# Gated product in its own tile, partial sums in `u`, and w_down's work tied to rounds, in a one-core encoder block

## The chip, the cores and the metric

One core of a Trainium2 chip runs the whole program. The metric is the time of one execution on the device in microseconds, the median of several runs. Engines work through their own instruction lists in order and wait for each other by semaphores: TensorE (PE, matmuls), VectorE (DVE), ScalarE (ACT), GpSimd (POOL) and SyncE (SP), whose queue issues the DMAs of this kernel.

## The reference

One layer of a hybrid encoder: token mixing (convolution and attention in parallel), cross-attention into 256 memory tokens, and a gated MLP. Of these the change touches the seam between the cross-attention and the MLP, and the MLP:

```python
h = rmsnorm(x, norm_mem_pre); y = memory_cross_attention(h, mem_n, ...)
x = x + rmsnorm(y, norm_mem_post)
h = rmsnorm(x, norm_ffn_pre)                   # 1024 tokens x 1024
u = jnp.einsum("bsd,df->bsf", h, w_up)         # 1024 x 5632
u = dwconv_centred(u, ffn_dw, ffn_dw_b)        # three taps along the tokens
gate, val = u[..., :D_FF], u[..., D_FF:]       # D_FF = 2816
y = jnp.einsum("bsf,fd->bsd", jax.nn.gelu(gate, approximate=True) * val, w_down)
x = x + rmsnorm(y, norm_ffn_post)
```

All of it is float32; each matmul operand is split into a high and a low part, and a product is three matmuls (high-high, high-low, low-high).

## The kernel before

**The seam.** The last product of the cross-attention runs over 8 token tiles `t` (`cross_gemm`, result `y2` in PSUM). For each tile `cross_norm` makes the two norms: Square on ACT, `rt` and `rs` on POOL (L86, L87), scaling and residual on DVE (L623, L624), Square again, `rt` and `rs` again, and `h` (named `h3` in the code) on DVE (L725). `cross_operands` transposes `h` on PE (`pTs`) and forms from it the moving operands b11, b21, b22, t1 to t4 of the MLP, each with a split into high (`h`) and low (`l`) part; t1 to t4 need the second half of the tokens, thus tile 7.

**The up stage.** There are NF = 22 blocks of 128 gate and 128 value columns, one block a *round* `fi`. A round replaces eight half-products by seven (Strassen's scheme in Winograd's form), p1 to p7, each of 12 matmuls of 128x512. `up_first` makes p1 and p2 from the weights `wg`, split into `a1`; `up_operands` loads `wv`, makes sums `s12` and `s34` on POOL, and splits them into `a2`, `a3`, `a22`; `up_finish` makes p6, p5, p3, p7, p4 and adds them up on DVE into `u` (L836), convolves (`conv3`), applies gelu, and multiplies gate and value (L859) into `u[:, 1]`, which is stored to `act_d[fi]` in DRAM (L860). On PE p1 and p2 of round fi run ahead of p6 to p4 of round fi - 1. Rounds 0 and 1 have their p1 and p2 at the seam (`UP_PRE = 2`).

**w_down's sums.** The down product uses the same scheme on 2x2 blocks; its right-hand sums are made during the up stage: `down_load` loads a slice of w_down into `wd_b` (two slots), `down_sums` makes four subtractions on DVE (L769), `down_store` stores the slice to `T_d` in DRAM (L772).

**The down stage** (`yd`) makes seven products m1 to m7 over 11 pairs `i`; left operands are formed from `acts` (reloaded from act_d), right ones from `st` (a stage of w_down or T_d in a tmp or raw buffer, two `i` each); the split pair is `op`.

**Buffers.** Tiles come from rotating pools; a new tile waits until the last use of the old one is over. `wp` has 7 (a1, a2, a3, a22, u), `tmp` 4 (x2, h3, q, s12, s34), `raw` 3 (wg, wv, x1r), PSUM `psB` 4 banks for p1 to p7, pTs and some yd. The order of instructions on each engine is set by a scheduler that goes by dependencies and its own costs, not by the order in the source alone.

## Time and profile before

| | us |
|---|---|
| median of 3 runs (lowest, highest) | 1452.29 (1451.33, 1456.73) |
| the profiled execution | 1453.6 |
| its span, first to last instruction | 1451.5 |
| PE busy / DVE busy / ACT busy / POOL busy | 1383.5 / 1070.8 / 699.9 / 514.0 |
| first p1 of the up stage | 757.96 |
| first down matmul | 1230.53 |

The profiled execution has 2.1 us ahead of and behind its span. Times within the rows count from the start of the span. A busy PE is not a PE at full speed: the granted clock has two levels, 2.4 and 1.2 GHz, and stands in the windows as a share of the higher. Idle time ahead of an instruction is shown in square brackets with the instruction that ended it.

### The profile page before, as it was taken

To read this page: it belongs to the slowest core of one execution; us is meant where nothing else is said; L and a number is where in the kernel's file an instruction comes from. 1 tells how busy PE (TensorE), PEld (TensorE's weight loads), DVE (VectorE), ACT (ScalarE), POOL (GpSimd) and SP (SyncE) were. 2 spreads that over 40 slices of the span, in tenths; PEclk is the share of its full clock that TensorE was granted. 3 is DMA by queue.
4 is the path that set the end of the run, shared out by engine and by line. 5 is a ranking of instruction groups with operands and counts; after the bars stand their busy time and mean duration, and the time that the engine had idled before them with its cause. 6 is when DMAs were issued, how large, how long until landed. Compare 5 with 4: busy or idle time off the path is not lost.

```text
span 1451.5 us, 18836 instructions
## 1 busy us (share of the span) xinstructions
PE 1383.5 (95%) x7042; PEld 1167.5 (80%) x7042; DVE 1070.8 (74%) x1442; ACT 699.9 (48%) x1191; POOL 514.0 (35%) x506
## 2 busy tenths in 40 slices
PE   9999999799999999999996989789999999999996
PEld 7889988679898888888885767678888888888885
DVE  6699899799998334335458878877777778985576
ACT  7426543588888434334444424234444443544452
POOL 5548887600102324002136525345554441000003
PEclk9999999999999999999998999899999999999998
DMA  6417750000000434013223576742222228622325
GB/s 236 135 59 238 243 200 14 19 1 2 30 1 12 163 103 151 24 43 131 87 87 102 174 232 198 236 135 83 74 93 81 88 87 317 226 88 88 109 87 210
DMA packets 74060, 170.08 MB, mean 117 GB/s; under 512 B 9713, under 2 KB 32497, under 8 KB 73969
## 3 DMA queue, kind: packets, MB, share of 16 engines
q1 hardware_dynamic: 73968, 168.88, 35.1%
q8 instruction: 55, 0.90, 0.3%
q14 instruction: 37, 0.30, 0.1%
HBM read 124.82 MB, written 44.04 MB: 116 GB/s over the span
## 4 chain that ended last, share of the span: by engine, by line
PE 62%; DVE 7%; DMA 5%; ACT 2%; issue 2%; POOL 1%; POOLq 0%; DVEq 0%; ACTq 0%; SPq 0%
PE p L98 7%; PE p L99 6%; PE p L101 6%; PE yd L91 5%; PE yd L92 5%; PE yd L93 5%; PE y L99 4%; PE y L101 4%; PE y L98 4%; PE pPT L82 3%; DVE wd L769 3%; DMA wd<-in_w_down_dram 2%; DMA T_d<-wd 2%; PE sc L101 2%; PE sc L98 2%; PE sc L99 2%
## 5 line engine op out<-in xcount | busy, mean ns | idle before, releaser
L305 DVE SCALAR_TENSOR_TENSOR cacc<-conv,col,cacc 128x1009 f32<-128x1009 f32 (+14 forms) x120 | 145.8, 1276 | 4.7 <-ACT cacc L253 4.5
L86 POOL TENSOR_SCALAR rt<-ss 128x1 f32<-128x1 f32 (+1 forms) x43 | 15.0, 349 | 353.5 <-DVE ss L920 227.2
L92 PE MATMUL yd<-op 128*128 128x512 f32 x308 | 119.8, 389 | 0.0
L93 PE MATMUL yd<-op 128*128 128x512 f32 x308 | 119.7, 389 | 0.0
L775 ACT CAST a<-s 128x512 fp32r<-128x512 f32 x88 | 50.8, 621 | 105.6 <-PE p L101 65.1
L91 PE MATMUL yd<-op 128*128 128x512 f32 x308 | 96.9, 389 | 0.0
L930 ACT CAST op<-acts 128x512 fp32r<-128x512 f32 x77 | 48.0, 624 | 99.6 <-PE yd L93 87.8
L776 POOL TENSOR_TENSOR a<-wg,a 128x512 fp32r<-128x512 f32 x44 | 63.1, 1456 | 84.1 <-ACT a L775 84.0
L920 DVE TENSOR_TENSOR op<-acts,op 128x512 fp32r<-128x512 f32 x77 | 53.1, 690 | 46.5 <-ACT op L930 46.4
L826 DVE SCALAR_TENSOR_TENSOR c<-u,col,c 128x1023 f32<-128x1023 f32 x44 | 56.6, 1285 | 39.9 <-ACT c L825 39.9
L557 DVE TENSOR_TENSOR PL<-pPT,PH 128x512 fp32r<-128x512 f32 x128 | 83.2, 681 | 2.4 <-ACT PH L556 1.4
L539 DVE TENSOR_REDUCE nm<-sp 128x1 f32<-128x1024 f32 x64 | 78.0, 1218 | 7.3 <-PE sp L537 6.8
L825 ACT ACTIVATE c<-u,col 128x1024 f32<-128x1024 f32 x44 | 53.2, 1209 | 54.8 <-DVE u L836 53.4
L542 ACT ACTIVATE P<-sp,nm 128x1024 f32<-128x1024 f32 x64 | 72.2, 1128 | 15.4 <-PE pPT L82 6.5
L776 DVE TENSOR_TENSOR a<-s,a 128x512 fp32r<-128x512 f32 x88 | 67.0, 779 | 15.2 <-ACT a L775 15.0
L556 ACT CAST PH<-pPT 128x512 fp32r<-128x512 f32 x128 | 69.4, 593 | 13.9 <-PE pPT L82 13.4
L769 DVE TENSOR_TENSOR wd<-wd 128x256 f32<-128x256 f32 x88 | 57.0, 664 | 20.5 <-DMA wd<-in_w_down_dram 20.0
L82 PE MATMUL pPT<-ident,P 128*128 128x128 f32 x512 | 67.9, 273 | 0.7 <-DVE PL L557 0.7
L92 PEld LDWEIGHTS yd<-op 128*128 128x128 f32 x308 | 57.8, 188 | 12.4 <-DVE op L920 0.4
L91 PEld LDWEIGHTS yd<-op 128*128 128x128 f32 x308 | 57.8, 188 | 12.0
L93 PEld LDWEIGHTS yd<-op 128*128 128x128 f32 x308 | 57.8, 188 | 12.0
L776 POOL TENSOR_TENSOR a<-wv,a 128x512 fp32r<-128x512 f32 x22 | 32.9, 1513 | 97.5 <-ACT a L775 83.1
(344 smaller groups left out, 4395.1 us busy)
## 6 DMA issues: line engine op xcount, KB each, us to landing
wg<-in_w_up_dram SPq DMA_DIRECT2D x22, 512.0 KB, 4.4
wv<-in_w_up_dram SPq DMA_DIRECT2D x22, 512.0 KB, 4.2
wd<-in_w_down_dram SPq DMA_DIRECT2D x22, 512.0 KB, 4.2
T_d<-wd SPq DMA_DIRECT2D x22, 512.0 KB, 3.9
act_d<-u SPq DMA_DIRECT2D x22, 512.0 KB, 2.9
acts<-act_d SPq DMA_DIRECT2D x22, 512.0 KB, 6.8
st<-T_d SPq DMA_DIRECT2D x20, 512.0 KB, 3.7
wmkv_r<-in_w_mkv_dram SPq DMA_DIRECT2D x16, 512.0 KB, 4.1
```

The source lines that it names most:

```text
L82: nc.tensor.transpose(out=out_, in_=in_, identity=ident)
L91: nc.tensor.matmul(out=ps, lhsT=sh, rhs=mh, start=first, stop=False)
L92: nc.tensor.matmul(out=ps, lhsT=sh, rhs=ml, start=False, stop=False)
L93: nc.tensor.matmul(out=ps, lhsT=sl, rhs=mh, start=False, stop=last)
L98: nc.tensor.matmul(out=p, lhsT=sh, rhs=mh, start=first, stop=False)
L99: nc.tensor.matmul(out=p, lhsT=sh, rhs=ml, start=False, stop=False)
L101: ins = nc.tensor.matmul(out=p, lhsT=sl, rhs=mh, start=False, stop=last)
L305: nc.vector.scalar_tensor_tensor(out=acc[:, t0:t1_], in0=a[:, t0 + o:t1_ + o], scalar=cc(C_DW + c * 31 + j), in1=acc[:, t0:t1_], op0=ALU.m ...
L539: nc.vector.reduce_max(out=nm, in_=sp, axis=AX.X, negate=True)
L557: nc.vector.tensor_tensor(out=PL[dst], in0=p3, in1=f(PH[dst]), op=ALU.subtract)
L769: nc.vector.tensor_tensor(out=dst, in0=in0, in1=in1, op=ALU.subtract)
L776: eng.tensor_tensor(out=dst[:, 1, :], in0=src, in1=f(dst[:, 0, :]), op=ALU.subtract)
```

## The change

- The product of gate and value goes into a tmp tile `o`, from which it is stored; `u` has its last use in that multiplication.
- The partial sums `q` lie in the second half of `u` instead of a tmp tile.
- w_down: the load of a round is issued behind the load of that round's `wv`; its four sums go behind the addition of p7 of the round ahead (`issue_after`), its store behind a later load of the w_up weights.
- The `wv` of rounds 0 and 1 are loaded into one tile `wv2` of the w pool ahead of the last tile's norm; the splits of `a1` for rounds 0 and 1 and the sums of round 0 come ahead of it as well; that norm gets high priority; the subtraction t3 of tile 7 moves from POOL to DVE.

```diff
@@ -624,9 +624,11 @@
         nc.vector.tensor_tensor(out=t, in0=t, in1=resid, op=ALU.add)
         return t
 
+    last_load = [None]
+
     def load_raw(src, name):
         r = raw(name)
-        nc.sync.dma_start(out=r, in_=src)
+        last_load[0] = nc.sync.dma_start(out=r, in_=src)
         return r
 
@@ -715,7 +717,7 @@
-    def cross_norm(t, y, xr):
+    def cross_norm(t, y, xr, eng=None):
...
     def cross_operands(t, j):
+        third = nc.gpsimd if t < 7 else nc.vector
         h, tt = t // 4, t % 4
         ts_ = slice(tt * 128, tt * 128 + 128)
         if t == 4:
@@ -743,7 +746,7 @@
             b_sub("t1", "b12", "b11", ts_, nc.vector)
             b_split("t1", ts_)
             b_split("b22", ts_)
-            b_sub("t3", "b22", "b12", ts_, nc.gpsimd)
+            b_sub("t3", "b22", "b12", ts_, third)
             b_sub("t2", "b22", "t1", ts_, nc.vector)
             b_split("t2", ts_)
             b_split("t3", ts_)
@@ -761,19 +764,22 @@
         return dr[fi // 2, :, :, fi % 2 * 256:fi % 2 * 256 + 256]
 
     def down_load(fi):
-        nc.sync.dma_start(out=wd_b[:, fi % 2], in_=down_slice(w_down, fi))
-
-    def down_sums(fi):
+        with tc.issue_after(last_load[0].ins):
+            nc.sync.dma_start(out=wd_b[:, fi % 2], in_=down_slice(w_down, fi))
+
+    def down_sums(fi, behind):
         b11, b12, b22, b21 = [wd_b[:, fi % 2, b, :] for b in range(4)]
-        for dst, in0, in1 in ((b11, b12, b11), (b12, b22, b12), (b22, b22, b11), (b21, b22, b21)):
-            nc.vector.tensor_tensor(out=dst, in0=in0, in1=in1, op=ALU.subtract)
+        with tc.issue_after(behind.ins):
+            for dst, in0, in1 in ((b11, b12, b11), (b12, b22, b12), (b22, b22, b11), (b21, b22, b21)):
+                nc.vector.tensor_tensor(out=dst, in0=in0, in1=in1, op=ALU.subtract)
 
     def down_store(fi):
-        nc.sync.dma_start(out=down_slice(T_d, fi), in_=wd_b[:, fi % 2])
+        with tc.issue_after(last_load[0].ins):
+            nc.sync.dma_start(out=down_slice(T_d, fi), in_=wd_b[:, fi % 2])
 
     def a_split(dst, src, eng):
         nc.scalar.copy(out=dst[:, 0, :], in_=src)
-        eng.tensor_tensor(out=dst[:, 1, :], in0=src, in1=f(dst[:, 0, :]), op=ALU.subtract)
+        return eng.tensor_tensor(out=dst[:, 1, :], in0=src, in1=f(dst[:, 0, :]), op=ALU.subtract)
 
     def product(ps, a, b):
         bh, bl = BO[b]
@@ -785,39 +791,56 @@
     H0, H1 = slice(0, 512), slice(512, 1024)
     ups, firsts, rgs = {}, {}, {}
 
-    def up_first(fi):
-
+    a1s, rvs, sums = {}, {}, {}
+    UP_PRE = 2
+
+    def up_first_operands(fi):
         rg = rgs.pop(fi) if fi in rgs else load_raw(w_up[fi, 0], "wg")
         a1 = W([2, 2, 512], "a1")
         a_split(a1[:, 0], rg[:, H0], nc.gpsimd)
         a_split(a1[:, 1], rg[:, H1], nc.gpsimd)
+        a1s[fi] = rg, a1
+
+    def up_first(fi):
+
+        if fi not in a1s:
+            up_first_operands(fi)
+        rg, a1 = a1s[fi]
         u = wp.tile([128, 2, 1024], F32, tag="w", name="u")
-        q = tmp("q")
+        q = u[:, 1, :]
         p1, p2 = psB("p1"), psB("p2")
         product(p1, a1[:, 0], "b11")
         nc.scalar.copy(out=q[:, H0], in_=p1)
         product(p2, a1[:, 1], "b21")
         nc.vector.tensor_tensor(out=u[:, 0, H0], in0=p2, in1=q[:, H0], op=ALU.add)
-        firsts[fi] = (rg, u, q)
-
-    def up_operands(fi):
-
-        rg, u, q = firsts.pop(fi)
-        rv = load_raw(w_up[fi, 1], "wv")
+        firsts[fi] = (u, q)
+
+    def up_sums(fi):
+        rg, _ = a1s.pop(fi) if fi >= UP_PRE else a1s[fi]
+        rv = rvs.pop(fi) if fi in rvs else load_raw(w_up[fi, 1], "wv")
         s12, s34 = tmp("s12"), tmp("s34")
         nc.gpsimd.tensor_tensor(out=s12[:, H0], in0=rv[:, H0], in1=rv[:, H1], op=ALU.add)
         nc.gpsimd.tensor_tensor(out=s12[:, H1], in0=s12[:, H0], in1=rg[:, H0], op=ALU.subtract)
         nc.gpsimd.tensor_tensor(out=s34[:, H0], in0=rg[:, H0], in1=rv[:, H0], op=ALU.subtract)
         nc.gpsimd.tensor_tensor(out=s34[:, H1], in0=rg[:, H1], in1=s12[:, H1], op=ALU.subtract)
+        sums[fi] = rv, s12, s34
+
+    def up_operands(fi):
+
+        if fi not in sums:
+            up_sums(fi)
+        rv, s12, s34 = sums.pop(fi)
+        u, q = firsts.pop(fi)
         a2, a3 = W([2, 2, 512], "a2"), W([2, 2, 512], "a3")
         a_split(a2[:, 0], s12[:, H1], nc.vector)
         a_split(a2[:, 1], s12[:, H0], nc.vector)
         a_split(a3[:, 0], s34[:, H1], nc.vector)
-        a_split(a3[:, 1], s34[:, H0], nc.vector)
+        lo = a_split(a3[:, 1], s34[:, H0], nc.vector)
         if fi % 2 == 0:
             a22[0] = W([2, 2, 512], "a22")
         a_split(a22[0][:, fi % 2], rv[:, H1], nc.gpsimd)
         ups[fi] = (a2, a3, a22[0][:, fi % 2], u, q)
+        return lo
 
     def conv3(fi, gv, u):
         ci = gv * NF + fi
@@ -833,7 +856,7 @@
         a2, a3, a22_, u, q = ups.pop(fi)
 
         def add(dst, ps, other, op=ALU.add, swap=False):
-            nc.vector.tensor_tensor(out=dst, in0=other if swap else ps, in1=ps if swap else other, op=op)
+            return nc.vector.tensor_tensor(out=dst, in0=other if swap else ps, in1=ps if swap else other, op=op)
 
         p6, p5 = psB("p6"), psB("p5")
         if fi == 0:
@@ -848,24 +871,37 @@
         add(u[:, 0, H1], p3, q[:, H1])
         p7 = psB("p7")
         product(p7, a3[:, 1], "t3")
-        add(q[:, H0], p7, q[:, H0])
+        seventh = add(q[:, H0], p7, q[:, H0])
         add(u[:, 1, H1], p5, q[:, H0])
+        if fi + 1 < NF:
+            down_sums(fi + 1, seventh)
         cg = conv3(fi, 0, u)
         nc.scalar.activation(out=u[:, 0], in_=cg, func=AF.Gelu_apprx_tanh)
         p4 = psB("p4")
         product(p4, a22_, "t4")
         add(u[:, 1, H0], p4, q[:, H0], op=ALU.subtract, swap=True)
         cv = conv3(fi, 1, u)
-        nc.vector.tensor_tensor(out=u[:, 1], in0=u[:, 0], in1=cv, op=ALU.mult)
-        nc.sync.dma_start(out=act_d[fi], in_=u[:, 1])
-
-    UP_PRE = 2
+        o = tmp("o")
+        nc.vector.tensor_tensor(out=o, in0=u[:, 0], in1=cv, op=ALU.mult)
+        nc.sync.dma_start(out=act_d[fi], in_=o)
+
     for t in range(8):
         if t == 6:
             for fi in range(UP_PRE):
                 rgs[fi] = load_raw(w_up[fi, 0], "wg")
-        j = cross_norm(t, *cross_gemm(t))
-        if t == 7:
+        y, xr = cross_gemm(t)
+        if t < 7:
+            j = cross_norm(t, y, xr)
+        else:
+            wv2 = wp.tile([128, 2, 1024], F32, tag="w", name="wv2")
+            for fi in range(UP_PRE):
+                last_load[0] = nc.sync.dma_start(out=wv2[:, fi], in_=w_up[fi, 1])
+                rvs[fi] = wv2[:, fi]
+            for fi in range(UP_PRE):
+                up_first_operands(fi)
+            up_sums(0)
+            with tc.high_priority():
+                j = cross_norm(t, y, xr)
             for fi in range(UP_PRE):
                 up_first(fi)
         cross_operands(t, j)
@@ -873,16 +909,15 @@
         if fi < NF:
             if fi >= UP_PRE:
                 up_first(fi)
-            up_operands(fi)
-        if fi == 0:
-            down_load(0)
+                down_store(fi - 2)
+            lo = up_operands(fi)
+            down_load(fi)
+        if fi:
+            up_finish(fi - 1)
         else:
-            down_store(fi - 1)
-            up_finish(fi - 1)
-        if fi < NF:
-            down_sums(fi)
-        if fi + 1 < NF:
-            down_load(fi + 1)
+            down_sums(0, lo)
+    for fi in (NF - 2, NF - 1):
+        down_store(fi)
```

How the order moves, at three places. First POOL around the last two norms; before, `a1_7359` is a1 of round 0, `rs_7258` the second norm of tile 6, and the rows with `7345` and `7355` are tile 7's two norms:

```order
L776 TENSOR_TENSOR a1_7359<-wg_7191,a1_7359 128x512 x2
L86 TENSOR_SCALAR rt1_7260<-ss_7257 128x1
L87 TENSOR_TENSOR rs_7258<-rt1_7260,mhalf_82 128x1
L86 TENSOR_SCALAR rt1_7345<-ss_7342 128x1
L87 TENSOR_TENSOR rs_7343<-rt1_7345,mhalf_82 128x1
L711 TENSOR_TENSOR r_b12_7058<-r_b22_7059,r_b12_7058 128x4x128
L86 TENSOR_SCALAR rt1_7355<-ss_7352 128x1
L87 TENSOR_TENSOR rs_7353<-rt1_7355,mhalf_82 128x1
L776 TENSOR_TENSOR a1_7394<-wg_7193,a1_7394 128x512 x2
```

and now, with `a1_7344` and `a1_7349` for rounds 0 and 1, and the same `rs_7258` of tile 6:

```order
L782 TENSOR_TENSOR a1_7344<-wg_7191,a1_7344 128x512 x2
L822 TENSOR_TENSOR s12_7354<-wv2_7341 128x512
L824 TENSOR_TENSOR s34_7355<-wg_7191,wv2_7341 128x512
L86 TENSOR_SCALAR rt1_7260<-ss_7257 128x1
L782 TENSOR_TENSOR a1_7349<-wg_7193,a1_7349 128x512 x2
L823 TENSOR_TENSOR s12_7354<-s12_7354,wg_7191 128x512
L87 TENSOR_TENSOR rs_7258<-rt1_7260,mhalf_82 128x1
L825 TENSOR_TENSOR s34_7355<-wg_7191,s12_7354 128x512
L86 TENSOR_SCALAR rt1_7364<-ss_7361 128x1
L87 TENSOR_TENSOR rs_7362<-rt1_7364,mhalf_82 128x1
L713 TENSOR_TENSOR r_b12_7058<-r_b22_7059,r_b12_7058 128x4x128
L86 TENSOR_SCALAR rt1_7374<-ss_7371 128x1
```

Between the a1 of round 0 and tile 6's `rs` there now stand two sums, the two splits of round 1's a1 and one more sum; before, only `rt` stood there.

Second DVE in an early round (before: round 4's additions into `q_7889`), from the addition of p6 to that of p7. In the whole round, up to the next addition of p6, 14 sums `wd` stand there; in the round ahead of it, 11:

```order
L836 TENSOR_TENSOR q_7889<-p6_8085,q_7889 128x512
L769 TENSOR_TENSOR wd_6644<-wd_6644 128x256
L776 TENSOR_TENSOR a2_8072<-s12_8066,a2_8072 128x512 x2
L769 TENSOR_TENSOR wd_6644<-wd_6644 128x256 x2
L836 TENSOR_TENSOR q_7889<-p5_8086,q_7889 128x512
L776 TENSOR_TENSOR a3_8073<-s34_8067,a3_8073 128x512
L769 TENSOR_TENSOR wd_6644<-wd_6644 128x256
L776 TENSOR_TENSOR a3_8073<-s34_8067,a3_8073 128x512
L769 TENSOR_TENSOR wd_6644<-wd_6644 128x256
L836 TENSOR_TENSOR u_7888<-p3_8113,q_7889 128x512
L769 TENSOR_TENSOR wd_6644<-wd_6644 128x256
L836 TENSOR_TENSOR q_7889<-p7_8127,q_7889 128x512
```

and now, in a round of the same stretch, where the partial sums are in `u_8175`:

```order
L859 TENSOR_TENSOR u_8175<-p6_8372,u_8175 128x512
L782 TENSOR_TENSOR a2_8359<-s12_8353,a2_8359 128x512
L859 TENSOR_TENSOR u_8175<-p5_8373,u_8175 128x512
L782 TENSOR_TENSOR a2_8359<-s12_8353,a2_8359 128x512
L782 TENSOR_TENSOR a3_8360<-s34_8354,a3_8360 128x512 x2
L859 TENSOR_TENSOR u_8175<-p3_8400,u_8175 128x512
L849 SCALAR_TENSOR_TENSOR c_8433<-u_8175,col_84,c_8433 128x1023
L859 TENSOR_TENSOR u_8175<-p7_8414,u_8175 128x512
L774 TENSOR_TENSOR wd_6644<-wd_6644 128x256
L851 SCALAR_TENSOR_TENSOR c_8433<-u_8175,col_84,c_8433 128x1023
L859 TENSOR_TENSOR u_8175<-p5_8373,u_8175 128x512
L774 TENSOR_TENSOR wd_6644<-wd_6644 128x256
```

The sums of w_down are gone from between the additions of p6, p5, p3 and p7; four stand behind p7 in every round.

Third DVE at the turn to the down stage. `op_10661` (`op_10660` in the change) is the operand for i = 2 of m1, its lower half made from `st`; `u_10362` (`u_10358`) is the last round's. Before, from the addition of p7:

```order
L836 TENSOR_TENSOR q_10363<-p7_10542,q_10363 128x512
L920 TENSOR_TENSOR acts_10594<-acts_10594 128x512
L920 TENSOR_TENSOR op_10661<-acts_10586,op_10661 128x512
L920 TENSOR_TENSOR op_10661<-st_10659,op_10661 128x512
L826 SCALAR_TENSOR_TENSOR c_10557<-u_10362,col_84,c_10557 128x1023
L836 TENSOR_TENSOR u_10362<-p5_10501,q_10363 128x512
L836 TENSOR_TENSOR u_10362<-q_10363,p4_10562 128x512
L920 TENSOR_TENSOR op_10678<-acts_10588,op_10678 128x512
L920 TENSOR_TENSOR acts_10586<-acts_10586 128x512
L920 TENSOR_TENSOR op_10678<-st_10659,op_10678 128x512
```

and now, where the row `op_10660<-st_10658` stands behind the last product `o_10576`; the addition of p7 stands 16 rows ahead of this piece:

```order
L849 SCALAR_TENSOR_TENSOR c_10572<-u_10358,col_84,c_10572 128x1023
L955 TENSOR_TENSOR op_10713<-acts_10591,op_10713 128x512
L851 SCALAR_TENSOR_TENSOR c_10572<-u_10358,col_84,c_10572 128x1023
L955 TENSOR_TENSOR op_10713<-st_10694,op_10713 128x512
L955 TENSOR_TENSOR acts_10591<-acts_10591 128x512
L955 TENSOR_TENSOR op_10732<-acts_10593,op_10732 128x512
L885 TENSOR_TENSOR o_10576<-u_10358,c_10572 128x1024
L955 TENSOR_TENSOR acts_10599<-acts_10599 128x512
L955 TENSOR_TENSOR acts_10593<-acts_10593 128x512
L955 TENSOR_TENSOR op_10749<-acts_10595,op_10749 128x512
L955 TENSOR_TENSOR op_10660<-st_10658,op_10660 128x512
L955 TENSOR_TENSOR op_10677<-st_10658,op_10677 128x512
```

The half made from `st` moved from ahead of the last round's convolution to behind its last multiplication. On SyncE the load of that `st` moved behind the last store to T_d.

## Rows read from the trace of the kernel before

**Rows 1.** The page: span, and busy time of each engine.
```profile
span 1451.5 us, 18836 instructions
...
PE 1383.5 (95%) x7042; PEld 1167.5 (80%) x7042; DVE 1070.8 (74%) x1442; ACT 699.9 (48%) x1191; POOL 514.0 (35%) x506
```

**Rows 2.** Windows: length, busy of PE, PEld, DVE, ACT, POOL, granted clock, DMA.
```profile
767.76:773.84 6.08, 6.08 (x18) 5.07 (x19) 4.21 (x4) 4.73 (x9) 5.23 (x4) 0.51 0.20 75
1100.00:1120.00 20.00, 20.00 (x90) 16.58 (x89) 14.68 (x18) 8.26 (x12) 6.92 (x6) 1.00 0.24 79
1220.00:1240.00 20.00, 20.00 (x90) 16.57 (x89) 19.93 (x28) 8.76 (x12) 0.00 (x0) 1.00 0.99 372
```

**Rows 3.** Timeline of PE: start, length, instruction, idle time ahead and releaser.
```profile
757.14 1.06 PE L82 MATMUL pTs<-ident,h 128*128 128x128 f32 x8 [1.06 <-DVE h L725]
...
767.76 0.79 PE L98 MATMUL p<-b11h,a 128*128 128x512 f32 x1 [4.08 <-ACT a L775]
...
769.63 1.91 PE L82 MATMUL pTs<-ident,h 128*128 128x128 f32 x8
...
784.50 0.79 PE L101 MATMUL p<-t1h,a 128*128 128x512 f32 x1 [5.06 <-DVE a L776]
...
798.90 0.47 PE L98 MATMUL p<-t4h,a 128*128 128x512 f32 x1 [2.31 <-DVE q L836]
...
988.45 0.39 PE L98 MATMUL p<-b11h,a 128*128 128x512 f32 x1
...
1007.49 0.39 PE L98 MATMUL p<-b11h,a 128*128 128x512 f32 x1
...
1230.53 0.39 PE L91 MATMUL yd<-op 128*128 128x512 f32 x1
```

**Rows 4.** Waits of PE, 757 to 980: total, times, longest.
```profile
PE p L98 <- ACT a L775: 21.8, 7, 5.7
PE p L98 <- DVE q L836: 6.1, 5, 2.3
...
PE p L98 <- DVE u L836: 3.1, 2, 1.8
```

**Rows 5.** Waits of all engines, 745 to 980.
```profile
ACT a L775 <- DMA act_d<-u: 33.0, 6, 10.8
...
DVE wd L769 <- DMA wd<-in_w_down_dram: 20.0, 11, 5.0
```

**Rows 6.** Groups of instructions, VectorE, 800 to 955.
```profile
L769 DVE TENSOR_TENSOR wd<-wd 128x256 f32<-128x256 f32 x81 | 50.7, 639 | 20.5 <-DMA wd<-in_w_down_dram 20.0
```

**Rows 7.** Waits of SyncE's DMA queue, 738 to 980.
```profile
SPq L772 <- DVE wd L769: 44.6, 14, 8.4
```

**Rows 8.** Timeline of POOL and DVE around the last norms.
```profile
750.06 3.98 POOL L776 TENSOR_TENSOR a<-wg,a 128x512 fp32r<-128x512 f32 x2
...
773.48 1.75 POOL L808 TENSOR_TENSOR s<-wv 128x512 f32<-128x512 f32 x1
...
789.77 1.29 POOL L808 TENSOR_TENSOR s<-wv 128x512 f32<-128x512 f32 x1
...
751.11 1.78 DVE L708 TENSOR_TENSOR t1l<-r_b,t1h 128x512 fp32r<-128x512 f32 x1
...
755.72 1.27 DVE L725 SCALAR_TENSOR_TENSOR h<-x,rs,gG 128x1024 f32<-128x1024 f32 x1
...
784.37 2.48 DVE L708 TENSOR_TENSOR t4l<-r_b,t4h 128x512 fp32r<-128x512 f32 x4
...
792.78 5.37 DVE L769 TENSOR_TENSOR wd<-wd 128x256 f32<-128x256 f32 x6
```

**Rows 9.** Timeline of DVE at the turn to the down stage.
```profile
1231.30 1.28 DVE L826 SCALAR_TENSOR_TENSOR c<-u,col,c 128x1023 f32<-128x1023 f32 x1
...
1246.89 0.69 DVE L920 TENSOR_TENSOR op<-acts,op 128x512 fp32r<-128x512 f32 x1
1247.49 1.22 DVE L859 TENSOR_TENSOR u<-u,c 128x1024 f32<-128x1024 f32 x1
```


## The prediction

> **What bounds the kernel now.** I read the page first. TensorE is busy in 1383.5 us of a span of 1451.5 [rows 1], so a gain must come from idle or slow TensorE time. The windows of 20 us then show where that is: between 757 and 980, where the up-projection of the MLP starts. In the steady part behind it PE is busy 20.00 of 20.00 with VectorE at 14.68 [rows 2], and one round (one ff block, 84 matmuls) lasts from 988.45 to 1007.49, 19.04 us [rows 3].
>
> From p4 of round 0 at 798.90 to the first down matmul at 1230.53 are 431.6 us [rows 3]. The work in it is 22 x 84 matmuls less the 96 ahead of it (p1 and p2 of rounds 0 and 1, four products of round 0), 1752, at 19.04 us for 84: 397.1 us. So 34.5 us are stalls and slow clock, all ahead of 988, since later rounds take exactly 19.04.
>
> The waits of PE name their owners [rows 4]: 21.8 us on ScalarE's cast into `a`, 6.1 and 3.1 on VectorE's additions. ScalarE in turn waited 33.0 us, six times, for the store of act_d out of `u` [rows 5]: a buffer of the w pool came free only once that store had landed. VectorE spent 50.7 us between 800 and 955 on 81 sums of w_down and 20.5 us idle ahead of them [rows 6], nearly all waiting for their loads [rows 5]. SyncE's queue stood 44.6 us before stores of T_d, waiting for those sums [rows 7], and the act_d stores stand in that queue. So w_down's work, bunched into the first rounds, holds up additions, stores and buffers.
>
> After a gap the clock is low too: behind the gap of 4.08 us the granted clock was 0.51 (the 1.2 GHz level) for 6.08 us [rows 2, 3], in which 10 matmuls and 8 transposes ran that cost 10 x 0.2267 + 1.06 = 3.3 us otherwise. Such a gap costs 2.8 us more.
>
> **Steady rounds.** Three edits meet here: `o` frees `u` with the multiplication instead of the store; sums inside `u` free one tmp buffer per round; w_down's work comes to four sums, one load and one store per round. VectorE in a round: 14.68 x 19.04/20 = 14.0 us, plus 4 sums at 0.639 [rows 6], 2.6: 16.6 of 19.04. It fits, but leaves only 2.4. Before, in the program's order, 11 to 14 sums stood between two p6 additions of the rounds from 3 on, 7 to 9 us. The new wait of POOL's s12 on an `o` store has two rounds of room; one act_d store and one w_down load per round leave the queue mostly idle. I take 32.5 of the 34.5 as gained, 2 staying for one low-clock stretch in the first rounds. Bounds: 34.5 (all goes), and 25.3 if the waits on VectorE's additions stay (34.5 - 6.1 - 3.1).
>
> **Start.** Here the change adds a wait. The POOL rows of the change show five operations between the two splits of a1(0) and `rs` of token tile 6: two sums, two splits of a1(1), one sum. The nearest rows are 1.29, 1.75 and 1.99 (3.98 for two) [rows 8]; five are 6.5 to 10.0 us, and I take 8, since VectorE is as busy beside them as beside the 1.75. Behind `rs` stands h of tile 6, which was at 755.72, and behind it the transposes on which PE waits: they go from 757.14 [rows 3] to about 765. Tile 7's Square writes the buffer that h of tile 6 reads, so its norm goes late too, but is covered: PE now has all 48 matmuls of the first two rounds between the two transposes, 10.9 us, and 2.8 for the low clock after the long gap. So the transposes of tile 7 end near 780; before, at 771.5 (769.63 and 1.91 [rows 3]).
>
> From there, before, t4l ended at 786.85 (784.37 and 2.48), 15.3 us behind those transposes; that chain contained splits stretched by POOL's sums, which now lie ahead. I take 11 us, t3's subtraction on VectorE (0.6) among them: t4l ends near 791. The w_down loads still wait for it; they landed 5.9 us later (first sum 792.78), and 4 sums instead of 6 (5.37 us x 4/6 = 3.6) and the addition that frees p4's PSUM bank (0.8, what is left to 798.90) follow [rows 3, 8]: p4(0) at 801.3, 2.4 us later than the 798.90 of before. Bounds: 805.6 with the old 15.3 us (+6.7), and 798.2 (-0.7) if the loads don't hold p4: p5 then starts as before at 784.50, 48 matmuls take 10.9 and a low-clock stretch 2.8.
>
> A split that ran beside POOL took 1.78 us at 751.11 [rows 8], against 0.69 for that size with POOL empty [rows 9]. The Trainium skill (SBUF — State Buffer, Who interferes with whom) says that a VectorE operation with two SBUF inputs and a GpSimd operation that reads SBUF block each other for a whole instruction. The stretch of 1.1 us agrees. By that rule all five POOL operations would run at the longest price, +2 us on the start and a sum of 1437 instead of 1435, so it speaks against sums ahead of the norm.
>
> **Turn to the down stage.** Call the first down matmul E. Before, it came without a stall, PE 20.00 and VectorE 19.93 of 20.00 [rows 2]. In the new order the lower half of the weight operand for i = 2 (`op` from `st`) stands behind the whole last round on VectorE, the product `o` included; before, it stood ahead of that round's gate convolution. Its load moved behind the last T_d store. The last p7 ends 12 matmuls ahead of E, at E - 2.7; its addition takes 0.6. From there to the end of that split are 26 VectorE instructions: 4 convolution steps at 1.28, 2 products at 1.22, 20 short ones at 0.60 (1246.89 to 1247.49) [rows 9], 19.6 us. It ends at E + 17.5. PE has the 24 matmuls of i = 0 and 1 until then, 5.4 us: 12.1 us idle, with 2.8 for the clock 14.9. I take 13, since some of the short gaps of that chain leave the clock high. Bounds: 0 (the old turn, with a VectorE as full, had no stall) and 18 (14.9 and three waits on ScalarE inside that chain, an estimate of 1 us each from the 1.28 of a step). What follows of the down stage is unchanged and PE-bound.
>
> **Sum.** +2.4 - 32.5 + 13 = -17.1 us. Against the profiled execution, 1453.6 us (span 1451.5, 2.1 around it), that is 1436.5; this execution lies 1.3 over the median of 1452.3, so I predict 1435.
>
> **Rivals.**
> The turn costs nothing: -30.1, 1422. For it speaks that VectorE was as full in the old turn; against it that the row now stands behind the last product by program order.
> Everything goes to its bad end: +6.7 - 25.3 + 18 = -0.6, 1452; partly so, 1444 to 1452.
> The buffer wait only changes place (POOL's sums wait for an `o` store, casts wait for POOL): the 21.8 us stay, +2.4 - 12.7 + 13 = +2.7, 1455. For it: the stores remain in one queue. Against: two rounds of slack.
> Slower: VectorE waits in every round at the first sum for its load, in order, with the convolution behind it. Waits of this kind were 20.0 us over 11, 1.8 each [rows 5]; 20 rounds of it give +36, so +19, 1471. It decides against the change once a round is stretched by 17.1/20 = 0.86 us. Against it: the load is issued a round ahead.
> The start gains as well: from 757.14 to 798.90 PE needs 96 matmuls and 16 transposes, 23.4 us of 41.8; without the 18.4 the sum is -37.9, 1414. Against it: POOL's order.
>
> **How the numbers follow.** Chances: as summed, 1428 to 1444, 0.55; free turn, 0.12; bad ends, 0.15; moved wait, 0.05; slower, 0.06; better start, 0.07. The range 1420 to 1450 leaves out the last two, part of the moved wait and the worst of the bad ends. A measurement here tells about 0.5%, 7.3 us, from no change: under 1445 lie the first two, the better start and a little of the bad ends: 0.76 faster; slower is the stretched round and a little of the moved wait, 0.06; the rest, 0.18, is the same.
>
> **What would show it.** In the profile after: PE idle some 8 us ahead of the transposes of tile 6, with POOL's `rs` late; no wait on the cast into `a` behind 810, no wait of ScalarE on act_d; first down matmul near 1200; there a wait of PE on VectorE's or ScalarE's `op` of 8 us or more. I am wrong if rounds behind 810 are longer than 19.04, if the transposes of tile 6 stay near 757, or if the turn has no gap.

## The result and the profile after

The changed kernel takes 1445.53 us (median of 10 runs, 1442.5 to 1449.93) against 1454.1 us for the kernel before on the same chips: ratio 0.9939, 95% interval 0.992 to 0.9957. The ratio makes it 8.9 us (0.0061 x 1454.1), the difference of the medians is 8.6; about 17 were forecast.

The page of the changed kernel, span and engines:

```profile
span 1445.5 us, 18853 instructions
...
PE 1380.5 (96%) x7042; PEld 1169.1 (81%) x7042; DVE 1103.9 (76%) x1443; ACT 701.0 (48%) x1191; POOL 522.1 (36%) x505
```

VectorE (DVE) is 33 us busier than in [rows 1] with one instruction more, so nearly the same work took longer. To find where the time went I cut the span at three matmuls: the last one of the token tiles' products y, the first one of p4 of round 0, and the first down matmul (`yd`). The first of them before:

```profile
755.47 0.61 PE L101 MATMUL y<-Uw,Pl 128*128 128x512 f32 x2
```

PE's timeline in the changed kernel (start, length, instruction, idle time ahead and releaser), to be held against [rows 3]:

```profile
757.21 0.61 PE L101 MATMUL y<-Uw,Pl 128*128 128x512 f32 x2
...
768.26 1.94 PE L82 MATMUL pTs<-ident,h 128*128 128x128 f32 x8 [10.44 <-DVE h L727]
...
781.74 1.03 PE L82 MATMUL pTs<-ident,h 128*128 128x128 f32 x8
...
790.24 0.80 PE L98 MATMUL p<-t1h,a 128*128 128x512 f32 x1 [7.47 <-ACT t1h L709]
...
809.11 0.64 PE L98 MATMUL p<-t4h,a 128*128 128x512 f32 x1 [4.70 <-DVE u L859]
...
1207.94 0.39 PE L91 MATMUL yd<-op 128*128 128x512 f32 x1
...
1214.21 0.50 PE L91 MATMUL yd<-op 128*128 128x512 f32 x1 [3.06 <-DVE u L859]
...
1219.01 0.80 PE L91 MATMUL yd<-op 128*128 128x512 f32 x1 [2.88 <-DVE u L859]
...
1227.51 2.08 PE L91 MATMUL yd<-op 128*128 128x512 f32 x4 [5.57 <-ACT op L965]
```

Four stretches follow from these times and the spans:

| stretch (us) | before | after | difference | forecast |
|---|---|---|---|---|
| up to the last y | 755.5 | 757.2 | +1.7 | 0 |
| start: last y to p4(0) | 43.4 | 51.9 | +8.5 | +2.4 |
| steady: p4(0) to first yd | 431.6 | 398.8 | -32.8 | -32.5 |
| down: first yd to the end | 221.0 | 237.6 | +16.6 | +13 |
| span | 1451.5 | 1445.5 | -6.0 | -17.1 |

The first line is no edit's: in the other kernels below the last y lies between 753.6 and 757.3. The profiled execution of the change, 1447.3 us, lies 1.8 over its median, and that of before 0.5 under, so the spans differ by less than the medians. The steady part came out as forecast; the start lost 6.1 us more and the turn 3.6 more.

The windows of the changed kernel (length, busy of PE, PEld, DVE, ACT, POOL, granted clock, DMA), against [rows 2]:

```profile
768.26:772.88 4.62, 4.62 (x18) 4.01 (x19) 2.87 (x4) 3.32 (x6) 2.04 (x3) 0.63 0.33 110
790.24:795.50 5.26, 4.71 (x10) 3.42 (x11) 5.26 (x10) 2.28 (x4) 0.00 (x0) 0.50 0.00 0
809.11:812.00 2.89, 2.89 (x7) 2.33 (x8) 2.86 (x4) 1.21 (x1) 2.81 (x3) 0.52 0.54 181
1100.00:1120.00 20.00, 20.00 (x90) 16.54 (x89) 18.33 (x21) 7.40 (x10) 14.43 (x11) 1.00 0.40 132
1219.01:1221.90 2.89, 2.89 (x6) 1.83 (x6) 2.82 (x4) 2.32 (x3) 0.00 (x0) 0.50 0.31 126
1227.51:1232.60 5.09, 5.09 (x12) 4.03 (x13) 3.55 (x6) 1.60 (x3) 0.00 (x0) 0.51 0.90 303
```

In the windows behind five gaps the granted clock is at or near its 1.2 GHz level, 0.50 to 0.63; behind the sixth, of 3.06 us at 1214.21, it was 0.81 over the next 1.99 us. In the steady part PE is full at 1.00, with VectorE at 18.33 of 20.

PE's waits from 740 to 1260, against [rows 4]:

```profile
PE pTs L82 <- DVE h L727: 10.4, 1, 10.4
PE p L98 <- ACT t1h L709: 7.5, 1, 7.5
PE yd L91 <- DVE u L859: 5.9, 2, 3.1
PE yd L91 <- ACT op L965: 5.6, 1, 5.6
PE p L98 <- DVE u L859: 4.7, 1, 4.7
```

The 21.8 us on casts into `a` are gone. In their place stand six long waits, three in the start and three at the turn, the earliest at the transposes of tile 6. POOL and VectorE there, against [rows 8]:

```profile
751.81 3.99 POOL L782 TENSOR_TENSOR a<-wg,a 128x512 fp32r<-128x512 f32 x2
755.75 1.73 POOL L822 TENSOR_TENSOR s<-wv 128x512 f32<-128x512 f32 x1
757.45 1.70 POOL L824 TENSOR_TENSOR s<-wg,wv 128x512 f32<-128x512 f32 x1
759.24 0.51 POOL L86 TENSOR_SCALAR rt<-ss 128x1 f32<-128x1 f32 x1
759.83 3.27 POOL L782 TENSOR_TENSOR a<-wg,a 128x512 fp32r<-128x512 f32 x2
763.06 1.71 POOL L823 TENSOR_TENSOR s<-s,wg 128x512 f32<-128x512 f32 x1
764.73 0.99 POOL L87 TENSOR_TENSOR rs<-rt,mhalf 128x1 f32<-128x1 f32 x1
...
782.33 1.65 POOL L824 TENSOR_TENSOR s<-wg,wv 128x512 f32<-128x512 f32 x1 [1.23 <-PE pTs L82]
...
785.62 3.38 POOL L782 TENSOR_TENSOR a<-wv,a 128x512 fp32r<-128x512 f32 x2
```
```profile
765.84 2.28 DVE L727 SCALAR_TENSOR_TENSOR h<-x,rs,gG 128x1024 f32<-128x1024 f32 x1
...
783.38 4.49 DVE L782 TENSOR_TENSOR a<-s,a 128x512 fp32r<-128x512 f32 x3
787.80 2.54 DVE L713 TENSOR_TENSOR r_b<-r_b,r_b 128x512 f32<-128x512 f32 x2
...
797.06 2.50 DVE L710 TENSOR_TENSOR t4l<-r_b,t4h 128x512 fp32r<-128x512 f32 x4
...
803.68 4.68 DVE L774 TENSOR_TENSOR wd<-wd 128x256 f32<-128x256 f32 x4 [4.12 <-DMA wd<-in_w_down_dram]
```

`rs` of tile 6 ends at 765.72, behind seven large operations of 1.64 to 2.0 us, and h behind it takes 2.28 us where it took 1.27. Ahead of t1 of tile 7 stand three splits at 1.50 each and two subtractions at 1.27; beside them POOL makes the last two sums of round 1 and the splits of its `a22`.

VectorE at the turn, against [rows 9]:

```profile
1208.76 0.68 DVE L859 TENSOR_TENSOR u<-p,u 128x512 f32<-128x512 f32 x1
...
1213.48 0.67 DVE L859 TENSOR_TENSOR u<-p,u 128x512 f32<-128x512 f32 x1
...
1218.28 0.67 DVE L859 TENSOR_TENSOR u<-u,p 128x512 f32<-128x512 f32 x1
...
1225.02 1.22 DVE L885 TENSOR_TENSOR o<-u,c 128x1024 f32<-128x1024 f32 x1
...
1227.96 1.29 DVE L955 TENSOR_TENSOR op<-st,op 128x512 fp32r<-128x512 f32 x2
```

The first row is the last round's addition of p7, the fourth its product, and the fifth begins with the lower half of the weight operand for i = 2. The second and third are the last round's additions of p5 and p4, and PE's waits of 3.06 and 2.88 us end with them. The program's pools suggest why: the four `yd` tiles of m1 come from the same four banks of `psB` as the last round's products, so a bank has to wait until its product has been added. ScalarE, which makes the upper halves of the operands, waits for the same last product:

```profile
1226.32 0.62 ACT L965 CAST op<-acts 128x512 fp32r<-128x512 f32 x1 [3.73 <-DVE o L885]
```

### The profile page after: what moved, and what is told of

Read it like the earlier page. It is cut to its first block, busy times and chain, and to the rows that moved or that the text cites. A ratio compares the mean times of both kernels' runs of the same rounds, so it can differ in the third digit from the quotient of the medians.

```text
span 1445.5 us, 18853 instructions
## 1 busy us (share of the span) xinstructions
PE 1380.5 (96%) x7042; PEld 1169.1 (81%) x7042; DVE 1103.9 (76%) x1443; ACT 701.0 (48%) x1191; POOL 522.1 (36%) x505
## 4 chain that ended last, share of the span: by engine, by line
PE 67%; DVE 6%; issue 2%; ACT 2%; DMA 1%; POOL 0%; SPq 0%; DVEq 0%; POOLq 0%; ACTq 0%
PE p L98 8%; PE p L99 8%; PE p L101 8%; PE yd L91 5%; PE yd L92 5%; PE yd L93 5%; PE y L99 4%; PE y L101 4%; PE y L98 4%; PE pPT L82 3%; PE sc L101 2%; PE sc L98 2%; PE sc L99 2%; PE sp L536 2%; PE po L567 2%
## 5 line engine op out<-in xcount | busy, mean ns | idle before, releaser
L86 POOL TENSOR_SCALAR rt<-ss 128x1 f32<-128x1 f32 (+1 forms) x43 | 10.9, 254 | 368.9 <-DVE ss L955 243.9
L92 PE MATMUL yd<-op 128*128 128x512 f32 x308 | 121.3, 394 | 0.0
L93 PE MATMUL yd<-op 128*128 128x512 f32 x308 | 121.2, 394 | 0.0
L91 PE MATMUL yd<-op 128*128 128x512 f32 x308 | 102.6, 396 | 11.5 <-DVE u L859 5.9
L782 POOL TENSOR_TENSOR a<-wg,a 128x512 fp32r<-128x512 f32 x44 | 68.2, 1571 | 73.1 <-ACT a L781 73.0
L782 DVE TENSOR_TENSOR a<-s,a 128x512 fp32r<-128x512 f32 x88 | 89.0, 1051 | 1.5 <-ACT a L781 1.5
L91 PEld LDWEIGHTS yd<-op 128*128 128x128 f32 x308 | 58.5, 190 | 25.9 <-DVE u L859 7.5
L859 DVE TENSOR_TENSOR u<-p,u 128x512 f32<-128x512 f32 x110 | 75.0, 683 | 5.6 <-PE p L101 4.5
L556 ACT CAST PH<-pPT 128x512 fp32r<-128x512 f32 x128 | 69.4, 594 | 14.6 <-PE pPT L82 14.1
L774 DVE TENSOR_TENSOR wd<-wd 128x256 f32<-128x256 f32 x88 | 67.6, 768 | 4.9 <-DMA wd<-in_w_down_dram 4.1
L92 PEld LDWEIGHTS yd<-op 128*128 128x128 f32 x308 | 58.7, 191 | 12.6 <-DVE op L955 0.4
```

The lines of the kernel that those rows point to most:

```text
L91: nc.tensor.matmul(out=ps, lhsT=sh, rhs=mh, start=first, stop=False)
L92: nc.tensor.matmul(out=ps, lhsT=sh, rhs=ml, start=False, stop=False)
L93: nc.tensor.matmul(out=ps, lhsT=sl, rhs=mh, start=False, stop=last)
L782: return eng.tensor_tensor(out=dst[:, 1, :], in0=src, in1=f(dst[:, 0, :]), op=ALU.subtract)
L859: return nc.vector.tensor_tensor(out=dst, in0=other if swap else ps, in1=ps if swap else other, op=op)
```

## The experiments

Three questions: does the turn's loss belong to the tile `o`, or to VectorE being full and to w_down's late work; does the start lose by where POOL's work stands, or by how slowly it runs; and which of the edits gives the 33 us. The ratio is to the kernel before measured beside it; the stretches are cut as above, from one profiled execution each. The change, turn_u and st_raw have the same start in the program, and theirs took 51.9, 49.9 and 50.7 us, so a difference of 2 us in one stretch tells nothing.

| kernel | median us | ratio, interval | start | steady | down |
|---|---|---|---|---|---|
| before | 1454.1 | 1 | 43.4 | 431.6 | 221.0 |
| the change | 1445.53 | 0.9939 (0.992 to 0.9957) | 51.9 | 398.8 | 237.6 |
| turn_u | 1429.4 | 0.9824 (0.9805 to 0.9844) | 49.9 | 398.8 | 222.8 |
| start_old | 1436.95 | 0.9872 (0.9849 to 0.9895) | 44.1 | 397.5 | 237.3 |
| oq_only | 1463.14 | 1.0052 (1.0031 to 1.0072) | 45.2 | 423.2 | 236.3 |
| wd_only | 1446.11 | 0.994 (0.9918 to 0.9961) | 42.9 | 424.4 | 222.0 |
| both_undone | 1422.46 | 0.9786 (0.977 to 0.9803) | 44.0 | 397.7 | 222.8 |
| loads_only | 1424.72 | 0.9802 (0.9785 to 0.9819) | 47.5 | 399.1 | 222.9 |
| rs_first | 1431.39 | 0.9839 (0.9816 to 0.9862) | 49.6 | 397.9 | 223.2 |
| st_raw | 1439.65 | 0.9901 (0.9886 to 0.9916) | 50.7 | 399.0 | 231.1 |
| wd_o | 1442.84 | 0.9926 (0.9911 to 0.9941) | 42.8 | 401.6 | 241.6 |
| wd_q | 1430.34 | 0.9834 (0.9818 to 0.9851) | 49.3 | 400.2 | 224.5 |
| turn_sums0 | 1426.57 | 0.9812 (0.9797 to 0.9826) | 48.1 | 398.4 | 222.8 |
| no_sums | 1427.66 | 0.982 (0.9805 to 0.9835) | 47.4 | 397.6 | 222.8 |
| dve_start | 1419.87 | 0.9761 (0.9741 to 0.978) | 41.1 | 397.8 | 222.9 |
| dve_old_start | 1418.59 | 0.975 (0.973 to 0.977) | 39.1 | 398.3 | 222.7 |
| late_sums0 | 1424.08 | 0.9791 (0.9767 to 0.9814) | 43.8 | 398.3 | 222.7 |

### One part undone, or one alone

**turn_u**: the product of the last two rounds goes back into `u`.

```diff
-        o = tmp("o")
+        o = tmp("o") if fi < NF - 2 else u[:, 1]
```

> The changed kernel, with the product of the last two rounds in u again instead of a tmp tile. Theory: the stall at the turn to the down stage (16.6 us from the first down matmul to the end beside before) comes from the tmp tile o: the load of st for i = 2 can only go into a tmp buffer that an o of the last rounds held, and so stands behind its store. Then about 1430, no gap of PE over 2 us between the first down matmul and 20 us behind it. Rival: the turn is late because w_down's sums and stores now reach into the last rounds; then still 1445 with the same gaps.

Down 222.8 instead of 237.6, the time 16.1 us less. All that PE still waits between 1195 and 1270:

```profile
PE yd L92 <- DVE op L955: 1.3, 1, 1.3
```

The gap that PE had ahead of the operand is gone, and so are the two ahead of the banks. The two `o` tiles of the last rounds cause 14.8 of the 16.6 us of the turn. The other 1.8 are there without `o` too (1.0 in wd_only, 3.5 in wd_q, both below); I have not followed them.

**start_old**: wv loads, splits and sums behind the last norm, that norm without its priority, and t3 of tile 7 on POOL, all as before.

```diff
-        third = nc.gpsimd if t < 7 else nc.vector
+        third = nc.gpsimd
...
-        y, xr = cross_gemm(t)
-        if t < 7:
...
-                j = cross_norm(t, y, xr)
+        j = cross_norm(t, *cross_gemm(t))
+        if t == 7:
```

> The changed kernel with the start of before: wv, a1 and sums of rounds 0 and 1 are not put ahead of the last norm, t3 is on POOL; the other edits stay. Theory: the start loses 8.5 us through POOL's work ahead of rs of tile 6 and VectorE's splits ahead of t1; without it PE reaches the transposes of tile 6 some 9 us earlier, p4 of round 0 comes near 800, and the time is about 1437. Rival: p4 of round 0 is held by w_down's first loads and sums, which stay; then p4 is at 806 or later and the time 1443 to 1446.

Start 44.1 instead of 51.9, p4(0) at 800.16, the time 8.6 us less: all that the start lost comes from these edits of the start taken together.

**oq_only** is the kernel before with `o` and q in `u` alone.

> The kernel before with the tile o and the sums in u alone; w_down's work and the start as before. Theory: w_down's sums still crowd the first rounds, so of the 34.5 us of stalls 10 to 22 (the casts' waits for the act_d store) go, and the turn loses about 15 us as in the change, since the st row stands behind the last product: 1447 to 1459. Rival (the buffers are the whole gain of the up stage): 32 go, 15 lost, about 1437. Rival (w_down's order is the whole gain): nothing goes, about 1469.

Steady 423.2 (-8.4, less than the 10 to 22 expected), down 236.3 (+15.3): slower than before by 0.5%. The turn's loss comes with `o` when w_down's order is the old one, so that order and VectorE's sums are not its cause.

**wd_only** is start_old with q in a tmp tile and the product in `u`.

> The kernel before with w_down's load, sums and store tied to the rounds, alone: product in u, q a tmp tile, start as before. Theory: most of the stalls of the up stage go (20 to 33 us) since the act_d stores no longer stand behind T_d stores, and the turn loses nothing without o: 1421 to 1434. Rival (the buffers are needed): casts still wait for the act_d store in every round, 1440 or more. Rival (w_down's late sums cost the turn): a gap of 8 us or more at the turn, 1437 to 1450.

Steady 424.4 (-7.2), down 222.0: not the theory but its first rival, since ScalarE's wait for buffers stays in this kernel, 820 to 1200:

```profile
ACT a L781 <- DMA act_d<-u: 73.4, 15, 6.7
```

Alone, each half gives 7 to 8 of the 33 us.

**both_undone** is turn_u and start_old together.

> The start of before and the product of the last two rounds in u, together; steady rounds as in the change. Theory: the losses at the start (8.5 us) and at the turn (15 us) are apart and add up: 1437 less 15, 1420 to 1424, p4 of round 0 near 800, first down matmul near 1198, no gap behind it. Rival (one hides behind the other): 1428 or more.

1422.46: 23.1 us under the change, against 24.7 for the two apart (by the ratios 22.2 against 26.5). The two losses are nearly independent, and the steady gain needs neither the moved start nor `o` in the last two rounds.

### Which buffer the steady part needs

I held that both buffer edits are needed beside w_down's order. **wd_o** has `o` but q in a tmp tile; **wd_q** has q in `u` but the product in `u` too; both start as before.

> w_down tied to rounds and the product in its own tmp tile o, but the partial sums q in a tmp tile as before; start of before. Theory: o takes u out of the wait for its store, but needs a tmp buffer; with q, s12 and s34 that makes four a round in a pool of four, so POOL's sums wait for the stores of o and the steady part keeps 15 to 30 us of its stalls, and the turn loses 15 us: 1452 to 1467. Rival (o alone is what the steady part needs): as start_old, 1435 to 1439.

> w_down tied to rounds and the partial sums in u, but the product in u as before; start of before. Theory: u still waits for the act_d store, as in wd_only, so the casts keep holding PE in most rounds: 1442 to 1448, no loss at the turn. Rival (the tmp buffer that q gives back is what the steady part needs): 1420 to 1424.

Steady 401.6 and 400.2: either one does nearly all of it, and the theory falls. (The time of wd_q, 1430.34, is above its rival's too: its start took 49.3 us though the start's edits are not in it. The section Why the start lost comes back to that.) What each leaves over is hidden from PE: in wd_o POOL waits for a tmp buffer (820 to 1190),

```profile
POOL s L824 <- DMA act_d<-o: 113.3, 19, 15.7
```

in wd_q ScalarE for `u` (820 to 1200), never over 3.0 us, against 6.7 in wd_only:

```profile
ACT a L781 <- DMA act_d<-u: 22.6, 18, 3.0
```

wd_q has no `o`, and down is 224.5; wd_o has it, and down is 241.6. With q in `u`, then, `o` buys 2.7 us of the steady part (start_old's 397.5 against 400.2) and costs 12.8 of the down stage (237.3 against 224.5); in these two executions the start was 5.2 us shorter with it (44.1 against 49.3).

### How `o` reaches the turn

**st_raw** is the change with the first weight tiles `st` of the tmp pool taken from the raw pool.

```diff
-            st = (tmp if nst[0] % 2 == 0 else raw)("st").rearrange("p (i n) -> p i n", i=2)
+            st = (tmp if nst[0] % 2 == 0 and nst[0] > 3 else raw)("st").rearrange("p (i n) -> p i n", i=2)
```

> The changed kernel, with o in its tmp tile in all rounds, but st for i = 2 from the raw pool instead of the tmp pool. Theory: the stall at the turn comes from st having to follow the last o in the tmp pool; then most of the 15 us go: 1429 to 1434, no wait of PE for op of over 3 us in the first 20 us of the down stage. Rival: the stall comes from o's own place (the product or its store on the way of VectorE and of the queue), so it stays: 1442 to 1446.

The stall is smaller and elsewhere, at the first `st` that still comes from the tmp pool (i = 6). PE's timeline:

```profile
1212.87 0.50 PE L91 MATMUL yd<-op 128*128 128x512 f32 x1 [2.07 <-DVE u L859]
...
1231.59 0.80 PE L92 MATMUL yd<-op 128*128 128x512 f32 x1 [5.24 <-DVE op L955]
```

Down is 231.1: 6.5 of the 14.8 us come back, less than I had expected. Shown is that the stall follows the first `st` of the pool that `o` now uses, behind the last product. That it does so because the pool hands out its buffers in the order of the program is argued only.

### Why the start lost

**rs_first** is turn_u with the moved work behind `rs` of tile 6 in the order.

```diff
...
-            for fi in range(UP_PRE):
-                up_first_operands(fi)
-            up_sums(0)
+            with tc.issue_after(last_rs[0].ins):
+                for fi in range(UP_PRE):
+                    up_first_operands(fi)
+                up_sums(0)
```

> As turn_u, with all of the start's edits, but the splits of a1 and the sums are placed behind rs of tile 6 on POOL. Theory: tile 6's transposes come back to about 757 to 758 and the gap of 10.4 us goes; p4 of round 0 gains 5 to 9 us: 1420 to 1425. Rival: VectorE's and ScalarE's splits of a2 and a3 ahead of t1, and w_down's load behind t4l, set p4; the wait only moves, 1428 to 1430.

Tile 6's transposes are back at 754.17, and nothing is gained: start 49.6, and the median is 2.0 us over that of turn_u. The wait goes to tile 7, whose `rs` stands behind the same work:

```profile
754.17 1.06 PE L82 MATMUL pTs<-ident,h 128*128 128x128 f32 x8
...
784.86 1.94 PE L82 MATMUL pTs<-ident,h 128*128 128x128 f32 x8 [18.69 <-DVE h L728]
```

POOL's two `rs` of tile 7 in that kernel:

```profile
768.77 1.00 POOL L87 TENSOR_TENSOR rs<-rt,mhalf 128x1 f32<-128x1 f32 x1
...
781.85 0.55 POOL L87 TENSOR_TENSOR rs<-rt,mhalf 128x1 f32<-128x1 f32 x1
```

So a place a little further back does not help: POOL's work fits ahead of neither norm.

**loads_only** (turn_u without splits and sums ahead of the norm) and **no_sums** (turn_u without the sums alone) take parts of it away.

> As both_undone, but wv of rounds 0 and 1 are still loaded ahead of the last norm, which has its priority, and t3 of tile 7 stays on VectorE; splits of a1 and sums are not put ahead of the norm. Theory: loading early costs nothing and lets POOL's sums start earlier, while rs of tile 6 isn't behind them: p4 of round 0 at 796 to 800, 1416 to 1423. Rival (early loads are what hurts): 1428.

> As turn_u, with the loads of wv and the splits of a1 ahead of the last norm, but POOL's sums of round 0 not. Theory: POOL's work ahead of the norms of tiles 6 and 7 costs the start, by its amount; three sums less are 5 us: 1422 to 1426, tile 6's transposes near 758. Rival (the early loads, or the splits of a2 and a3 ahead of t1, cost it): 1428 to 1431.

Start 47.5 and 47.4 against 49.9 and, with everything as before, 44.0: both lie between, and neither theory nor rival came as stated. By these two traces the sums would be worth 2.5 us and the splits nothing, but the medians say otherwise: 1427.66 without the sums, within the noise of turn_u's 1429.4, and 1424.72 without the splits too, 3.3 us under the execution of loads_only that was profiled. The interval of loads_only overlaps that of both_undone as well. Which of the moved pieces costs how much is not shown.

**turn_sums0** (turn_u) and **late_sums0** (both_undone) put w_down's sums of round 0 behind p7 of round 0, so that they no longer stand ahead of the addition that frees p4's bank.

> As turn_u, with the w_down sums of round 0 behind the addition of p7 of round 0 instead of behind the last split. Theory: the 2 to 5 us that PE waits for p4 of round 0 are the first w_down load and its sums, in VectorE's order ahead of the additions that free p4's bank; without them 1425 to 1428 and no such wait. Rival (p4 is late for t4 anyway): 1429 to 1430.

> As both_undone, with the w_down sums of round 0 behind the addition of p7 of round 0. There PE waits 0.9 us for p4's bank, so theory: nothing that can be measured, 1421 to 1423. Rival (the sums between the first additions hold back more): 1418 to 1420.

Start 48.1 (-1.8) and 43.8 (-0.2). In turn_sums0 the wait for p4 is gone and the time, 1426.57, is where the theory had it, but the interval overlaps that of turn_u, and most of the late start stays: the wait for p4, 4.7 us in the change and 2.0 in turn_u, is the last link of a chain that is late already. In late_sums0 nothing is gained.

**dve_start** (turn_u) and **dve_old_start** (both_undone) keep every place in the text of the program and give the splits of a1 and the four sums of rounds 0 and 1 to VectorE.

```diff
-        a_split(a1[:, 0], rg[:, H0], nc.gpsimd)
-        a_split(a1[:, 1], rg[:, H1], nc.gpsimd)
+        eng = nc.vector if fi < UP_PRE else nc.gpsimd
+        a_split(a1[:, 0], rg[:, H0], eng)
+        a_split(a1[:, 1], rg[:, H1], eng)
...
-        nc.gpsimd.tensor_tensor(out=s12[:, H0], in0=rv[:, H0], in1=rv[:, H1], op=ALU.add)
...
+        eng.tensor_tensor(out=s12[:, H0], in0=rv[:, H0], in1=rv[:, H1], op=ALU.add)
...
```

> As turn_u (1429 us), with all of the start's edits, but the splits of a1 and the sums of rounds 0 and 1 on VectorE instead of POOL. Theory: the start costs through POOL's pace and what it does to VectorE's operations beside it (0.68 to 1.75 us); on VectorE the twelve operations take 0.7 us each and the stretching goes: tile 6's transposes near 760, p4 of round 0 at 798 to 801, 1421 to 1425. Rival: the work itself ahead of the norms costs, wherever it is done: 1428 to 1432.

> As both_undone (1422 us), with the splits of a1 and the sums of rounds 0 and 1 on VectorE instead of POOL. Theory (POOL's pace and the stretching of VectorE's operations cost the start of before as well): t3's splits take 2.5 us instead of 5.7, p4 of round 0 at 793 to 797, 1416 to 1420. Rival (VectorE is then too full): 1422 to 1426.

Start 41.1 and 39.1, 8.8 and 4.9 us less than with POOL, although VectorE now does 12 operations more. VectorE's four splits of t3 for tile 7 tell why; in both_undone, beside POOL's splits and sums, and in dve_old_start:

```profile
782.14 5.71 DVE L710 TENSOR_TENSOR t3l<-r_b,t3h 128x512 fp32r<-128x512 f32 x4
```
```profile
783.24 2.49 DVE L710 TENSOR_TENSOR t3l<-r_b,t3h 128x512 fp32r<-128x512 f32 x4
```

The same instructions take 1.43 us each beside a working POOL and 0.62 without. On VectorE the early place costs little: dve_start's start is 2.0 us longer than dve_old_start's and its median 1.3, within the noise, where with POOL the same place cost 5.9 of start (49.9 against 44.0) and 6.9 of the median. So what the start lost comes from that work being on POOL, by POOL's own pace and by the stretching of VectorE beside it; these two runs do not part the two.

A run that was made for something else shows the stretching alone. wd_q has the start of both_undone, and VectorE comes to the splits of t4 in the same order. But in wd_q POOL is already at the sums of round 2, from 793.23 on; in both_undone it is idle from 790.69 to 796.09 and begins those sums at 799.19. VectorE's next eight splits, in both_undone and in wd_q:

```profile
791.95 2.50 DVE L710 TENSOR_TENSOR t4l<-r_b,t4h 128x512 fp32r<-128x512 f32 x4
794.36 2.49 DVE L782 TENSOR_TENSOR a<-s,a 128x512 fp32r<-128x512 f32 x4
```
```profile
793.93 4.49 DVE L710 TENSOR_TENSOR t4l<-r_b,t4h 128x512 fp32r<-128x512 f32 x4
798.35 6.77 DVE L782 TENSOR_TENSOR a<-s,a 128x512 fp32r<-128x512 f32 x4
```

They take 11.3 us instead of 5.0, the addition that frees p4's bank stands behind them, PE waits 6.0 us for it, and the start is 5.3 us longer, though p4 needs none of those sums.

dve_old_start is the fastest kernel, 1418.59 us, ratio 0.975: the steady gain, the old start with its work on VectorE, and `o` only where it costs nothing.

## Why the prediction was right and wrong

**Steady: right in size, only partly in cause.** -32.5 forecast, -32.8 measured. No wait on the cast into `a` is left behind 812, and the VectorE load that I worked out for a round (16.6 of 19.04, or 17.4 of 20) is 18.33 of 20. I counted the buffer edits and w_down's order as one sum, and did not part them; the runs show that w_down's order with either buffer edit suffices.

**Start: the step that failed.** It was "that chain contained splits stretched by POOL's sums, which now lie ahead. I take 11 us". Taking off the 1.7 us by which this execution was late already, tile 6's transposes came at 766.5 (forecast 765) and tile 7's ended at 781.0 (forecast 780), so the cost of POOL's five operations was right. But from there t4l took 16.8 us, not 11, and not even the 15.3 of before, which I had as the bad bound. The sums of round 1 were still beside that chain, with the splits of a22, and the splits of a2 and a3 had come in ahead of t1: three at 1.50 us and two subtractions at 1.27, where the prices with POOL empty (0.69 in [rows 9], and 0.62 for a split of t4l above) give 3.3 us for the five instead of 7.0. That is 3.7 of the 5.8 us over my 11. The rest is about what I left out beside it: four more splits of a2 and a3 stood in that chain than before (three ahead of t1, two ahead of t3, where before one stood ahead of t4l), 0.6 us each even with POOL empty. Loads, sums and the addition behind t4l then took 9.6 us, near the 10.3 forecast.

The rule that the prediction weighed, in the Trainium skill (SBUF — State Buffer, Who interferes with whom), that a VectorE operation with two SBUF inputs and a GpSimd operation that reads SBUF block each other for a whole instruction, fits these rows: h at 2.28 beside POOL and 1.27 without, t3's splits at 1.43 and 0.62, and dve_start, where the same work without POOL gains. My mistake was to price it on POOL's five operations alone and to leave VectorE's own chain at prices without it.

**Turn: mechanism right for the wait that ends last, size off.** +13 forecast, +16.6 measured. The operand for i = 2 did stand behind the last product, and 26 VectorE instructions did lie between the addition of p7 and the end of that split: 19.2 us, forecast 19.6. What was mis-sized is the start of that chain: I let the addition begin with the end of p7, E - 2.7 (E is the first down matmul, now 1207.94). VectorE, as full as in the window at 1100, came to it at 1208.76, and it ended at E + 1.5 instead of E - 2.1. So the split ended at E + 20.7, forecast E + 17.5. PE needed 19.6 us for its first 24 matmuls where 5.4 would do, 14.1 lost, and the next twelve ran at 0.51 in 5.09 us instead of 2.7, 2.4 lost: 16.5. I had also taken 13 where my working gave 14.9. What I did not foresee at all is the two waits that end with the additions of p5 and p4, 3.06 and 2.88 us: the sign that I had named, one wait for `op` of 8 us or more, came as these two and 5.57 us for `op`. They lie ahead of the operand, which PE would have had to wait for without them, so they do not add to the sum. How the operand came to stand behind the product is, as said under st_raw, argued only.

**The chances.** Of the rivals none came as described. The nearest was the bad end with 0.15, 1444 to 1452, but the start went beyond its bound and the steady part had none of its loss. The time missed the likeliest band, 1428 to 1444, by 1.5 us and lies inside the range, and the 8.9 us against the median of before are 0.6%, just over the 0.5% named as the least that can be told; but that rests on the steady part alone, since start and turn gave back 25.1 us where I had 15.4.

## What to carry to other kernels

Price an elementwise operation that is moved ahead of a critical chain on both engines: by what it takes on POOL, and by what it adds to each VectorE instruction beside it, which can make the busier VectorE the cheaper place. A tile that frees one buffer earlier takes another from a pool that a later stage uses, so look at that pool's first tile behind the last round. Where an engine is over 90% busy its next instruction doesn't start when its input is ready: add its backlog to a chain. Here VectorE was at 92% (18.33 of 20), and the addition of p7 began 3.4 us behind its last matmul.

## What the runs showed of the hardware

- A 128x512 VectorE operation with two SBUF inputs took 0.62 to 0.69 us with POOL empty and 1.27 to 1.78 (the longest in [rows 8]) beside POOL's operations of the same size, which took 1.64 to 2.0 there. Even a 128x1 operation, POOL's `rs`, took 0.99 us at 764.73, and 0.55 at 781.85 of rs_first with VectorE idle.
- Where both engines stream such operations they move in step: in both_undone three of VectorE's begin at 774.12, 775.80 and 777.47 and three of POOL's at 773.60, 775.28 and 776.96, one each every 1.68 us. Alone, VectorE's follow each other every 0.60 us (2.50 for four) and POOL's every 1.22 (771.15 and 772.37), so together they are hardly faster than one behind the other, 1.82.
- Twelve operations moved from POOL to VectorE shortened the start by 8.8 us in one kernel and 4.9 in another: here VectorE alone was done with the work sooner than both engines sharing it.
- The granted clock was 0.50 to 0.63 in the windows shown, of 2.9 to 5.3 us, behind five gaps of 2.88 to 10.44 us. A gap's length alone does not settle it: behind 3.06 us it was 0.81 over 1.99 us, and behind the 2.88 us that followed 0.50.
